# Where in its tiles the normed stream of a two-layer hybrid decoder stands: at the start, or at the end

## Chip, core and metric

The kernel runs on one core of one Trainium2 chip. The metric is the device time of one execution in microseconds, the median of the runs shown; the profile is of one execution, with a time of its own.

## What is computed

The reference is a trunk of two decoder layers over 16 learned tokens and 256 positions (272 in all), 2048 wide, in float32. Each layer is a normed mixer and a normed gated feed-forward block with a causal convolution of width 3, both with a residual.

```python
def reference(...):
    h = concat(meta, x)                        # 272 positions
    for i in range(2):
        hn = rmsnorm(h, norm_mix[i])
        mix = mixer_ab(hn, ...) if i % 2 == 0 else mixer_cd(hn, ...)
        h = h + mix
        h = h + conv_ffn(rmsnorm(h, norm_ffn[i]), ffn_w_up[i], ffn_dw[i], ffn_w_down[i])
    return rmsnorm(h, norm_final)[:, 16:]

def conv_ffn(h, w_up, dw, w_down):
    u = causal_dwconv(h @ w_up, dw)
    val, gate = u[..., :5632], u[..., 5632:]
    return (silu(gate) * val) @ w_down
```

## The kernel before

The stream is held transposed: 16 tiles `h[m]` of 128 channels by 272 positions. A product takes a block of 128 x 128 weights as the stationary operand and up to 272 positions as the moving one. For accuracy both operands are split into a rounded high part and a rest: the weights, which SP fetches in tiles `wf` of 1024 columns, become `wh` (ACT, line 161) and `wl` (DVE or POOL, line 163), 512 columns each; and each step of a product is three matmuls, high by high (line 170), high by low (line 171) and low by high (line 172), added up in PSUM. `gemm_steps` holds this loop. One output block of the up projections takes 16 steps, so 48 matmuls.

`Norm` makes the moving operand. `make_x(m)` writes the gain times `h[m]` in two halves, high (ACT, line 213) and low (DVE, line 214), into one stretch of a slab: `x` for the first 13 of the 16 tiles, the second slab `lt` for the last three where the norm is "wide". The factor of the root mean square comes in later, when a product is read out of PSUM. `xs()` hands the halves to the products.

The layout has a rule, since both operands of a matmul are read from SBUF at the same time. Call the *distance* the column (of 4 bytes) at which the moving operand begins, less the one at which a weight block begins, modulo 64. All weight tiles are multiples of 64 columns, so every weight block begins at the same place modulo 64 (32 in the built program).

- The three wide norms (`norm_mix0` for the first mixer, `norm_ffn0` and `norm_ffn1` for the up projections) give each half XW = 320 columns, five times 64. All halves then begin at the same place modulo 64 (16): distance 48 for every matmul. `norm_mix0` and `norm_ffn0` hold 272 positions, `norm_ffn1` holds 258.
- The tiles `act` that the down projections read (272 positions in layer 0, 256 in layer 1) are put at the same distance by a tile `gap` of 48 columns that nothing uses.
- `norm_mix1`, for the second mixer, isn't wide: its halves are 272 columns apart, and their distances rotate. For an even tile the high half is at 48 and the low at 0, for an odd one at 16 and 32. A part of the products of this mixer skips the first 12 or 14 columns of each half.

No table or planner sets the order of instructions; it is that of the code, queue by queue. In the long products PE has the next weights ready while it computes, and the products of one stage follow each other without a gap.

Of the kernel before, what the change touches and what calls it, by code (L numbers as in the profile page):

```python
# [21 lines left out]
T = NM + SEQ  # L22
# [73 lines left out]
def _body(ctx, tc, nc, A):  # L96
# [16 lines left out]
    def slab2(dt):  # L113
        return xpool.tile([P, 8 * T + 16], dt, tag="lt", name="lt")

    def pc(name, i=0, r0=0, r1=P):
        o = PO[name] + i
        return par[r0:r1, o:o + 1]
# [32 lines left out]
    def gemm_steps(w, g, xs, kt, acc, pool_lo=(), load=LOADK):  # L151
        for k0 in range(0, kt, load):
            nk = min(load, kt - k0)
            wf = wpool.tile([P, LOADK * P], F32, tag="wf", name="wf", bufs=NWF)
            nc.sync.dma_start(wf[:, :nk * P], w[g, :, k0 * P:(k0 + nk) * P])
            for s0 in range(0, nk, SUB):
                ns = min(SUB, nk - s0)
                src = wf[:, s0 * P:(s0 + ns) * P]
                wh = wpool.tile([P, SUB * P], F32R, tag="wh", name="wh")
                wl = wpool.tile([P, SUB * P], F32R, tag="wl", name="wl")  # L160
                last_hi[0] = S.copy(wh[:, :ns * P], src)  # L161
                eng = G if (k0 + s0) // SUB in pool_lo else V
                lo = eng.tensor_sub(wl[:, :ns * P], src, wh[:, :ns * P].bitcast(F32))  # L163
                if eng is V:
                    last_lo[0] = lo
                for k in range(ns):
                    kk = k0 + s0 + k
                    xh, xl = xs[kk]
                    a, b = wh[:, k * P:(k + 1) * P], wl[:, k * P:(k + 1) * P]
                    PE.matmul(acc, a, xh, start=kk == 0, stop=False)  # L170
                    PE.matmul(acc, a, xl, start=False, stop=False)  # L171
                    PE.matmul(acc, b, xh, start=False, stop=kk == kt - 1)  # L172
                yield

    def gemm(w, g, xs, n, pool_lo=()):
        acc = psA.tile([P, T], F32, tag="acc", name="acc")
        for _ in gemm_steps(w, g, xs, len(xs), acc[:, :n], pool_lo):
            tick()
        return acc[:, :n]
# [5 lines left out]
    def parts(t, c0, c1):  # L185
        return t[:, 0, c0:c1], t[:, 1, c0:c1]
# [10 lines left out]
    class Norm:  # L197
# [5 lines left out]
        def make_x(self, m):  # L203
            hm = h[m][:, self.c0:]
            if m == NXW and self.wide:
                self.slab2 = slab2(F32R)

            w, slab, i = XW if self.wide else T, xslab, m
            if self.wide and m >= NXW:
                slab, i = self.slab2, m - NXW  # L210
            x = slab[:, 2 * w * i:2 * w * (i + 1)].rearrange("p (a t) -> p a t", a=2)
            xh, xl = parts(x, 0, self.n)
            S.activation(xh, hm, AF.Copy, scale=pc(self.g, m))
            V.scalar_tensor_tensor(xl, hm, pc(self.g, m), xh.bitcast(F32), op0=ALU.mult, op1=ALU.subtract)
            self.x.append(x)
# [24 lines left out]
            self.rstd = r[:, self.c0:]  # L240

        def xs(self):
            return [parts(x, 0, self.n) for x in self.x]

    def add_h(m, acc, c0):
        V.tensor_add(h[m][:, c0:], h[m][:, c0:], acc)
# [8 lines left out]
    def mixer_ab(tp):  # L255
        nm = Norm("norm_mix0", 0, tp)
# [4 lines left out]
        xs = []  # L261
        first = [psb()[:, :T] for _ in range(2)]
        steps = [gemm_steps(A["ab_in"], g, xs, KD, first[g], (), SUB) for g in range(2)]
        for a, b in ((0, 2), (2, 4), (4, 8), (8, 12), (12, 16)):
            nc.sync.dma_start(h0[:, a:b], A["hT"][:, a:b])
            for m in range(a, b):
                nm.make_x(m)
            xs.extend(parts(x, 0, T) for x in nm.x[a:])
            if b % SUB == 0:
                for st in steps:  # L270
                    next(st)
# [139 lines left out]
    def ffn(layer, nm, gname, c1, tp, feed, spill=None):  # L411
        nxt = Norm(gname, c1, tp)
        c0 = nm.c0
        tp.tile([P, ACT_GAP], F32, name="gap", bufs=1)
        n = T - c0
        pad = 2 if layer == 0 else 0
        no = n if layer == 0 else n - 2
        xs = nm.xs()
        up, down, dw = A["up%d" % layer], A["down%d" % layer], "ffn_dw%d" % layer
        for half in range(2):  # L420
            act = []
            for j in range(NFH):
                i = half * NFH + j
                res = []
                for q in range(2):
                    ps = gemm(up, 2 * i + q, xs, n)
                    nm.finish()
                    u = tp.tile([P, T + 16], F32, tag="u%d" % q, name="u")
                    if pad:
                        G.memset(u[:, 0:2], 0.0)  # L430
                    V.tensor_mul(u[:, pad:pad + n], ps, nm.rstd)
                    c = tp.tile([P, T], F32, tag="c%d" % q, name="c")
                    conv3(c[:, :no], u, no, dw, q * NF + i)
                    res.append(c[:, :no])
                silu = S.activation(res[1], res[1], AF.Silu)  # L435
                G.tensor_mul(res[0], res[0], res[1])  # L436
                d = tp.tile([P, 2, ACT_W[layer]], F32R, tag="act", name="act", bufs=24)
                split(d, res[0], no)
                act.append(parts(d, 0, no))
            warm(AF.Sqrt, [silu])  # L440
            for m in range(KD):
                add_h(m, gemm(down, half * KD + m, act, no), T - no)
                if half:
                    feed(nxt, m)
                    if spill is not None:
                        nc.sync.dma_start(spill[:, m, :], h[m])
        return nxt
# [5 lines left out]
    with tc.tile_pool(name="ab", bufs=2) as tp:  # L453
        nm = mixer_ab(tp)
    hs = dpool.tile([P, KD, T], F32, name="hs")
    with tc.tile_pool(name="ffn0", bufs=2) as tp:
        nm = ffn(0, nm, "norm_mix1", 0, tp, feed_x, hs)
# [581 lines left out]
    with tc.tile_pool(name="cd", bufs=2) as tp:  # L1039
        nm = mixer_cd(tp, nm)  # L1040
    with tc.tile_pool(name="ffn1", bufs=2) as tp:
# [10 lines left out]
        nm = ffn(1, nm, "norm_final", NM, tp, feed_out)  # L1052
# [109 lines left out]
```

## Time and profile before

| | us |
|---|---|
| median of three runs | 2467.48 (2464.82 to 2470.11) |
| the profiled execution, its own time | 2466.42 |
| its span, first to last instruction | 2464.6 |
| PE busy | 2435.1 |
| DVE busy | 1783.4 |
| ACT busy | 1332.8 |
| POOL busy | 543.3 |

Busy time of PE counts the time from a matmul's start to its modelled end, and successive matmuls overlap: a matmul of 272 columns has a row of some 287 ns, while the next one starts some 123 ns after it. How fast a stage goes is therefore read from the timeline, as the time between two starts that are many matmuls apart, divided by the number of intervals.

### The profile page before, as it was taken

Reading aid. Unit: us, or ns where it says so; the run is one execution under the profiler, and the core shown is the slowest. Engines: PE = TensorE matmul, PEld = TensorE weight load, DVE = VectorE, ACT = ScalarE, POOL = GpSimd, SP = SyncE. Lnnn points to the kernel's source line nnn. Section 1 sums busy time; section 2 is a strip of 40 time slices with the busy share of each in tenths; the row PEclk is TensorE's granted clock in tenths of the full one; section 3 lists DMA queues with packets and bytes.
Section 4 is the critical chain, followed back from the end, with each engine's and each line's share of the span. In section 5 each row is a group of like instructions: output and inputs, shape, how many; then the busy total and the mean of one; then the engine's idle time right before and its main releaser. Section 6 shows DMA issues by size and latency. Waiting matters only on the chain.

```text
span 2464.6 us, 53380 instructions
## 1 busy us (share of the span) xinstructions
PE 2435.1 (99%) x20476; PEld 2378.0 (96%) x20476; DVE 1783.4 (72%) x3399; ACT 1332.8 (54%) x2573; POOL 543.3 (22%) x790
## 2 busy tenths in 40 slices
PE   8999999999999999999999999999999999999998
PEld 8999999999999999999899988899999999999998
DVE  8897897776546777667786678889777655777754
ACT  5444665555445555556645445546555545555553
POOL 5676140000000000121248044414000000000022
PEclk9999999999999999999999999999999999999999
DMA  6555555555655555666456342245555566555564
GB/s 219 192 177 180 171 174 179 179 180 176 175 181 181 180 180 178 183 194 192 132 160 174 122 130 87 93 141 181 184 184 184 181 192 194 185 183 180 177 197 149
DMA packets 130990, 423.94 MB, mean 172 GB/s; under 512 B 18832, under 2 KB 27216, under 8 KB 130736
## 3 DMA queue, kind: packets, MB, share of 16 engines
q1 hardware_dynamic: 129824, 417.99, 53.1%
q8 instruction: 161, 2.64, 0.4%
q0 software_dynamic: 912, 2.55, 0.4%
q14 instruction: 93, 0.76, 0.1%
HBM read 414.41 MB, written 5.93 MB: 171 GB/s over the span
## 4 chain that ended last, share of the span: by engine, by line
PE 95%; DVE 2%; ACT 1%; DMA 1%; POOL 0%; issue 0%; SPq 0%; DVEq 0%; ACTq 0%; POOLq 0%
PE acc L170 30%; PE acc L172 30%; PE acc L171 30%; PE ps L901 1%; DVE ps L296 1%; PE ps L935 1%; DVE wl L163 0%; PE ps L916 0%; PE ps L950 0%; PE ps L803 0%; PE ps L958 0%; PE ps L964 0%; DMA wf<-ab_in 0%; PE ps L697 0%; DMA h<-hT 0%
## 5 line engine op out<-in xcount | busy, mean ns | idle before, releaser
L161 ACT CAST wh<-wf 128x512 fp32r<-128x512 f32 (+1 forms) x1576 | 956.1, 611 | 919.0 <-PE acc L171 800.0
L163 DVE TENSOR_TENSOR wl<-wf,wh 128x512 fp32r<-128x512 f32 (+1 forms) x1465 | 1027.9, 706 | 480.9 <-ACT wh L161 423.8
L170 PE MATMUL acc<-x,wh 128*128 128x272 f32 (+2 forms) x3582 | 1034.9, 289 | 1.7 <-ACT wh L161 1.7
L172 PE MATMUL acc<-x,wl 128*128 128x272 f32 (+2 forms) x3582 | 1024.3, 286 | 2.5 <-DVE wl L163 2.3
L171 PE MATMUL acc<-x,wh 128*128 128x272 f32 (+2 forms) x3582 | 1023.0, 286 | 0.0
L170 PEld LDWEIGHTS acc<-x,wh 128*128 128x128 f32 x3582 | 677.4, 189 | 15.9 <-issue 7.5
L172 PEld LDWEIGHTS acc<-x,wl 128*128 128x128 f32 x3582 | 677.3, 189 | 5.2 <-DVE wl L163 3.5
L171 PEld LDWEIGHTS acc<-x,wh 128*128 128x128 f32 x3582 | 677.9, 189 | 1.1 <-issue 0.3
L171 PE MATMUL acc<-act,wh 128*128 128x272 f32 (+1 forms) x1408 | 396.1, 281 | 0.0
L170 PE MATMUL acc<-act,wh 128*128 128x272 f32 (+1 forms) x1408 | 396.1, 281 | 0.0
L172 PE MATMUL acc<-act,wl 128*128 128x272 f32 (+1 forms) x1408 | 396.1, 281 | 0.0
L170 PEld LDWEIGHTS acc<-act,wh 128*128 128x128 f32 x1408 | 264.8, 188 | 0.0
L171 PEld LDWEIGHTS acc<-act,wh 128*128 128x128 f32 x1408 | 264.8, 188 | 0.0
L172 PEld LDWEIGHTS acc<-act,wl 128*128 128x128 f32 x1408 | 264.8, 188 | 0.0
L436 POOL TENSOR_TENSOR c<-c 128x272 f32<-128x272 f32 (+1 forms) x88 | 66.5, 756 | 639.9 <-ACT c L435 639.9
L170 PE MATMUL acc<-lt,wh 128*128 128x272 f32 (+1 forms) x642 | 183.4, 286 | 0.0
L171 PE MATMUL acc<-lt,wh 128*128 128x272 f32 (+1 forms) x642 | 182.9, 285 | 0.0
L172 PE MATMUL acc<-lt,wl 128*128 128x272 f32 (+1 forms) x642 | 182.9, 285 | 0.0
L163 POOL TENSOR_TENSOR wl<-wf,wh 128x512 fp32r<-128x512 f32 x111 | 149.1, 1353 | 54.2 <-ACT wh L161 53.5
L430 POOL MEMSET u<- 128x2 f32 x88 | 8.6, 100 | 573.1 <-DVE c L252 566.5
L172 PEld LDWEIGHTS acc<-lt,wl 128*128 128x128 f32 x642 | 121.7, 190 | 0.0
L171 PEld LDWEIGHTS acc<-lt,wh 128*128 128x128 f32 x642 | 121.6, 189 | 0.0
(316 smaller groups left out, 2858.2 us busy)
## 6 DMA issues: line engine op xcount, KB each, us to landing
wf<-up SPq DMA_DIRECT2D x352, 512.0 KB, 3.5
wf<-down SPq DMA_DIRECT2D x128, 512.0 KB, 3.7
wf<-cd_in SPq DMA_DIRECT2D x100, 512.0 KB, 3.6
wf<-ab_in SPq DMA_DIRECT2D x76, 512.0 KB, 3.7
wf<-down SPq DMA_DIRECT2D x64, 384.0 KB, 3.3
wf<-ab_out_s SPq DMA_DIRECT2D x16, 512.0 KB, 3.5
wf<-ab_out_a SPq DMA_DIRECT2D x16, 512.0 KB, 3.9
wf<-cd_out_o SPq DMA_DIRECT2D x16, 512.0 KB, 3.5
```

Source lines behind the costliest of these rows:

```text
L161: last_hi[0] = S.copy(wh[:, :ns * P], src)
L163: lo = eng.tensor_sub(wl[:, :ns * P], src, wh[:, :ns * P].bitcast(F32))
L170: PE.matmul(acc, a, xh, start=kk == 0, stop=False)
L171: PE.matmul(acc, a, xl, start=False, stop=False)
L172: PE.matmul(acc, b, xh, start=False, stop=kk == kt - 1)
L296: tap = V.scalar_tensor_tensor(c if t == 30 else run, ap[:, t:t + T], pc("conf_dw", 31 * i + t), run, op0=ALU.mult, op1=ALU.add)
L430: G.memset(u[:, 0:2], 0.0)
L436: G.tensor_mul(res[0], res[0], res[1])
L901: PE.matmul(gv[:, :128], bkc, t[r, h0], start=True, stop=True)
L935: PE.matmul(wy[H[h0], 0:64], t[:, h0, 0:64], sv[:, h0], start=True, stop=True)
```

## The change

The moving operand of the three wide norms stands at the end of its 320 columns, not at their start. `parts(x, a, b)` takes the columns a to b of both halves, and n is the number of positions that the norm holds (272 or 258).

```diff
@@ make_x
-            xh, xl = parts(x, 0, self.n)
+            xh, xl = parts(x, w - self.n, w)
             S.activation(xh, hm, AF.Copy, scale=pc(self.g, m))
             V.scalar_tensor_tensor(xl, hm, pc(self.g, m), xh.bitcast(F32), op0=ALU.mult, op1=ALU.subtract)
@@ xs
-            return [parts(x, 0, self.n) for x in self.x]
+            return [parts(x, x.shape[-1] - self.n, x.shape[-1]) for x in self.x]
@@ mixer_ab
-            xs.extend(parts(x, 0, T) for x in nm.x[a:])
+            xs.extend(nm.xs()[a:])
```

With 272 positions the first column moves by 48 columns (192 bytes), from distance 48 to distance 32; its columns from the 17th on, the last 256, begin at distance 48. With 258 positions the first column moves by 62 columns (248 bytes), to distance 46, and again the last 256 begin at distance 48. For `norm_mix1` w and n are both 272, and nothing moves. Tiles, their addresses and their sizes stay as they are, and so does the sequence of instructions on every engine (19130 listed ones on PE, 2637 on DVE, 1546 on ACT, 460 on POOL, 238 on SP): the change alters the start column of operands and nothing else.

## Rows read from the trace of the kernel before

**Rows 1.** The page: busy us (share) xinstructions; chain that ended last.
```profile
PE 2435.1 (99%) x20476; PEld 2378.0 (96%) x20476; DVE 1783.4 (72%) x3399; ACT 1332.8 (54%) x2573; POOL 543.3 (22%) x790
...
PE 95%; DVE 2%; ACT 1%; DMA 1%; POOL 0%; issue 0%; SPq 0%; DVEq 0%; ACTq 0%; POOLq 0%
PE acc L170 30%; PE acc L172 30%; PE acc L171 30%; PE ps L901 1%; DVE ps L296 1%; PE ps L935 1%; DVE wl L163 0%; PE ps L916 0%; PE ps L950 0%; PE ps L803 0%; PE ps L958 0%; PE ps L964 0%; DMA wf<-ab_in 0%; PE ps L697 0%; DMA h<-hT 0%
```

**Rows 2.** Waits of PE, longest first: us in total, times, longest us.
```profile
PE ps L170 <- ACT wh L161: 7.2, 2, 6.9
PE acc L172 <- DVE wl L163: 2.3, 4, 1.4
```

**Rows 3.** Stretches of 30 us: busy us of each engine (xinstructions), PEclk, DMA share, GB/s.
```profile
200.00:230.00 30.00, 30.00 (x246) 30.00 (x245) 24.27 (x50) 14.54 (x25) 21.70 (x17) 1.00 0.54 179
900.00:930.00 30.00, 30.00 (x246) 30.00 (x245) 21.45 (x39) 15.99 (x29) 2.05 (x7) 1.00 0.53 177
1800.00:1830.00 30.00, 30.00 (x253) 30.00 (x252) 21.63 (x39) 16.42 (x30) 1.48 (x2) 1.00 0.55 181
2000.00:2030.00 30.00, 30.00 (x268) 30.00 (x266) 16.59 (x29) 14.07 (x24) 0.00 (x0) 1.00 0.68 194
2200.00:2230.00 30.00, 30.00 (x251) 30.00 (x250) 21.16 (x38) 17.01 (x31) 1.91 (x3) 1.00 0.54 179
```

**Rows 4.** Timeline (start, duration us), PE, up projection of layer 0, 97 intervals.
```profile
900.02 0.29 PE L172 MATMUL acc<-lt,wl 128*128 128x272 f32 x1
...
911.98 0.28 PE L170 MATMUL acc<-lt,wh 128*128 128x272 f32 x1
```

**Rows 5.** Timeline, PE, up projection of layer 1, first half, 99 intervals.
```profile
1800.09 0.28 PE L172 MATMUL acc<-lt,wl 128*128 128x258 f32 x1
...
1811.97 0.28 PE L172 MATMUL acc<-lt,wl 128*128 128x258 f32 x1
```

**Rows 6.** Timeline, PE, up projection of layer 1, second half, 99 intervals.
```profile
2200.00 0.28 PE L172 MATMUL acc<-x,wl 128*128 128x258 f32 x1
...
2211.96 0.28 PE L172 MATMUL acc<-x,wl 128*128 128x258 f32 x1
```

**Rows 7.** Timeline, PE, down projection of layer 1, 105 intervals.
```profile
2000.08 0.28 PE L171 MATMUL acc<-act,wh 128*128 128x256 f32 x1
...
2011.98 0.28 PE L171 MATMUL acc<-act,wh 128*128 128x256 f32 x1
```

**Rows 8.** Timeline, PE, mixer of layer 1, rotating distances, 272 columns, 28 intervals.
```profile
1154.01 0.29 PE L170 MATMUL acc<-x,wh 128*128 128x272 f32 x1
...
1157.50 0.29 PE L171 MATMUL acc<-x,wh 128*128 128x272 f32 x1
```

**Rows 9.** Timeline, PE, mixer of layer 1, first 14 columns skipped, 32 intervals.
```profile
1211.27 0.28 PE L171 MATMUL acc<-x,wh 128*128 128x258 f32 x1
...
1215.12 0.28 PE L170 MATMUL acc<-x,wh 128*128 128x272 f32 x1
```

**Rows 10.** Weight loads by form: 2000 to 2030, 900 to 930, 1800 to 1830 us.
```profile
L170 PEld LDWEIGHTS acc<-act,wh 128*128 128x128 f32 x89 | 16.7, 188 | 0.0
...
L170 PEld LDWEIGHTS acc<-x,wh 128*128 128x128 f32 x66 | 12.4, 188 | 0.0
...
L170 PEld LDWEIGHTS acc<-x,wh 128*128 128x128 f32 x68 | 13.0, 191 | 0.0
```

**Rows 11.** Groups by form, whole span: busy us, mean ns, idle before, releasers.
```profile
L213 ACT ACTIVATE x<-h,par 128x272 fp32r<-128x272 f32 x42 | 21.0, 520 | 11.4 <-DVE h L246 5.9 <-DMA h<-hT 4.1
...
L214 DVE SCALAR_TENSOR_TENSOR x<-h,par,x 128x272 fp32r<-128x272 f32 x42 | 31.0, 753 | 5.0 <-ACT x L213 5.0
```

## The prediction

> **What bounds the kernel now.** I read the page's busy table and chain first. PE is busy for 99% of the span and 95% of the chain that ended last is PE, nearly all of it the three matmul lines 170, 171 and 172 [rows 1]. In the whole execution PE waits for other engines only in single pieces, the largest group being 7.2 us [rows 2]. So the time is a sum of intervals between the starts of successive matmuls, and an edit that moves no instruction can only act through that interval. A matmul's mean duration doesn't give it, because matmuls overlap: rows last 276 to 288 ns, but start every 113 to 125 ns. I therefore take the interval from the timeline, as first start to last start divided by the number of intervals. The granted clock is 1.00 in every stretch used, the 2.4 GHz level [rows 3], where 256 columns stream in 106.7 ns, 258 in 107.5 and 272 in 113.3.
>
> The intervals, in order of the stages [rows 4 to 9]:
> - 272 columns, up projection of layer 0: from 900.02 to 911.98 there are 97 intervals, 123.3 ns each, 10.0 above the streaming time [rows 4].
> - 258 columns, up projection of layer 1, first half: 1800.09 to 1811.97, 99 intervals, 120.0 ns, 12.5 above [rows 5].
> - the same in the second half: 2200.00 to 2211.96, 99 intervals, 120.8 ns, 13.3 above [rows 6].
> - 256 columns, down projection of layer 1: 2000.08 to 2011.98, 105 intervals, 113.3 ns, 6.7 above [rows 7].
>
> All four read their moving columns from the same distance to the weights (48 columns, counted modulo 64, from the start of a weight block to the first column). The two columns between 256 and 258 thus cost 6.7 to 7.5 ns [rows 5 to 7], where their streaming is 0.8. The weight load that runs beside the matmul lasts 188 ns beside 256 and 272 columns and 191 beside 258 [rows 10]: something delays these reads, and it isn't a semaphore. That is what the change can touch: if 272 and 258 paid only the 6.7 of 256, they would start every 120.0 and 114.2 ns.
>
> Two more stretches show other distances. In layer 1's mixer the normed tiles are 272 columns wide, so their halves rotate through all four distances (48, 0, 16, 32). There 272 columns take 124.6 ns (1154.01 to 1157.50, 28 intervals) [rows 8], and 258 columns that begin 14 columns into the tile take 120.3 ns (1211.27 to 1215.12, 32 intervals) [rows 9].
>
> **The change part by part.** It removes and adds no instruction, no wait and no transfer; sequences on all engines are the same. Two things change their address.
>
> (a) *The writers*, lines 213 and 214: 48 pairs on ACT and DVE, of the same shapes, at 520 and 753 ns for 272 columns [rows 11]. They write as many columns 192 or 248 bytes further on. 32 of the 48 pairs stand beside the last output projection of a mixer, where PE has work queued. The 16 of the first normalization stand at the start of the program, where the longest wait of PE is [rows 2]. A change of 5% in both would be 16 x 1.27 x 0.05 = 1 us; I take 0, and ±1 for the bounds.
>
> (b) *The readers*. Matmuls that read the moved tiles: 40 products of 16 steps and 3 matmuls in the first mixer (1920) and 88 x 16 x 3 = 4224 in the up projection of layer 0, so 6144 with 272 columns; and 4224 with 258 columns in that of layer 1. The rest (mixer of layer 1, both down projections, the output projections) reads tiles that don't move. For 272 columns the first column goes from distance 48 to distance 32. For 258 it goes from 48 to 46, in the middle of what was a 16-column step, so that the two extra columns now stand ahead of 256 columns at the common distance.
>
> No row shows all matmuls of a stage at distance 32 or 46, so the price is bounded from both sides.
> - 272 columns. Below: 120.0 ns, the extra cost of the 256-column rows. Above: 126.7, as far above the present 123.3 as 120.0 is below. I take the nearest row, the rotating stretch, in which one row in six is at distance 32: 124.6. That is +1.35 x 6144 = **+8.3 us**, with ends -20.5 and +20.5.
> - 258 columns. Below: 114.2 (-6.2 on the mean of 120.0 and 120.8, which is 120.4). Above: 123.7, the same 3.3 step. I take the rotating stretch whose rows also begin 14 columns past a 16-column step, 120.3, and leave the lock between the two halves open, so 120.6: +0.2 x 4224 = **+0.8 us**, ends -26.4 and +13.9.
>
> Cover: DVE has 21 to 24 busy of 30 us in these stages and the transfers 53 to 55% [rows 3], so a PE that gets 5% faster would still be fed; nothing hides a slower one, since PE has no idle time to give.
>
> Sum: 0 + 8.3 + 0.8 = +9.1 us on the profiled execution's 2466.4, that is 2475.5; the median of the runs shown is 1.06 us above that execution, so **2476.5**.
>
> **A rule weighed.** Rows 7 against rows 5 show that two columns more cost eight times their streaming time at an unchanged distance, and rows 8 against rows 4 that 272 columns cost 1.3 ns more when the distance rotates. The Trainium skill, "TensorE: Matmul & The Clock Gate", section "Step-by-step: what each phase is for", says the opposite of a cost by place: PE reads SBUF through two independent ports, one for the moving operand and one for weight loads, so a weight load takes no bandwidth from a running matmul. By it the sum would be 0 and the time 2467.5; this is the third rival below. The trace agrees with it only as far as both run at once.
>
> **The rivals.**
> 1. *Forecast: place matters, and the new place is no better than the mixed ones.* The present 48 is the one distance for which a stage of 272 columns runs in a regular beat of 123.3; leaving it costs what the rotating rows cost. Against it: in those rows each matmul follows one at another distance, so they don't show a beat at 32 alone. 2476.5, from +2 to +20 us. Chance 0.41.
> 2. *The tail is the cost (faster).* The present distance suits 256 columns [rows 7]; whatever comes behind the 256th column meets the weight load a further time. Ahead of them it doesn't. For: 256 to 258 is a step, not a slope [rows 5, 7], and the weight load grows with it at 258 [rows 10]. Against: beside 272 columns the load doesn't grow, and in rows 9 the 258 columns already begin 14 past a step, with their partial step ahead, and still take 120.3. It decides if 272 columns fall below 122.5 ns (-5 us). If only 272 gains: 2466.4 + 1.1 - 20.5 = 2447; if only 258: 2441; if both: 2421. Chance 0.29.
> 3. *Nothing.* The extra cost goes with the number of 16-column steps (16 for 256, 17 for both 258 and 272), which the move leaves as it is, or place doesn't matter. 2467.5 ± 4.9. Chance 0.20.
> 4. *Both stages fall out of their beat.* The first half of layer 1 runs in an even 120.0 and the second in 120.8 with the same addresses [rows 5, 6], so the beat isn't fixed by the addresses alone and can be lost: 126.7 and 123.7 give 2467.5 + 20.5 + 13.9 = 2502. Chance 0.10.
>
> **How the numbers follow.** Under 0.2% (4.9 us) either way can't be told from no change for this kernel. Slower: nearly all of the first (0.39) and the fourth: 0.49. Faster: 0.29. Within: 0.20 and the small end of the first: 0.22. The range reaches down to 2444, which holds the case where 272 alone gains and leaves out the larger gains (about 0.12), and up to 2496, which leaves out the full loss in both widths (about 0.08). The likeliest case's own range is 2469 to 2488.
>
> **What would show it.** In the profile after, the same stretches of the up projections, read as starts per interval: about 124.6 in layer 0 and 120.6 in layer 1 if I am right, 120.0 and 114.2 for the second rival, 123.3 and 120.4 for the third. The down projection of layer 1 must stay at 113.3 and the mixer of layer 1 near 124.6, since nothing there moved. I am wrong if the difference lies outside those 10368 matmuls, or if PE's waits in the start of the program change.

## The result: slower by 1.1%, three times the forecast loss

| | before | after |
|---|---|---|
| median, us | 2467.16 (2464.82 to 2470.11) | 2496.16 (2492.60 to 2496.76) |
| ratio, 95% interval | | 1.0111 [1.0098, 1.0124] |
| profiled execution / its span | 2466.42 / 2464.6 | 2492.6 / 2490.8 |

The forecast was 2476.5, so +9.1; the loss is 29.0, and the time lies at the very upper end of the range. The spans differ by 26.2 us.

The page of the changed kernel, busy time (share) x instructions and the chain that ended last:

```profile
span 2490.8 us, 53380 instructions
PE 2463.4 (99%) x20476; PEld 2406.8 (97%) x20476; DVE 1783.6 (72%) x3399; ACT 1336.5 (54%) x2573; POOL 542.6 (22%) x790
...
PE 97%; DVE 1%; ACT 1%; POOL 0%; DMA 0%; issue 0%; SPq 0%; DVEq 0%; POOLq 0%; ACTq 0%
```

Against [rows 1], PE has the same 20476 instructions and is busy 28.3 us longer; DVE, ACT and POOL stay within 4 us. PE's longest waits (total, times, longest) answer [rows 2]:

```profile
PE ps L170 <- ACT wh L161: 6.8, 1, 6.8
PE acc L171 <- DVE halves L183: 1.9, 1, 1.9
```

7.2 us became 6.8, so no wait of PE was added; the 1.9 us for DVE stands in the kernel before too. Most of the loss is in the pace. The stretches of 30 us of [rows 3], with the number of matmuls in brackets behind the first 30.00:

```profile
200.00:230.00 30.00, 30.00 (x239) 30.00 (x238) 24.93 (x52) 13.29 (x24) 20.97 (x17) 1.00 0.50 170
900.00:930.00 30.00, 30.00 (x239) 30.00 (x239) 20.96 (x38) 16.34 (x31) 2.82 (x8) 1.00 0.53 176
1800.00:1830.00 30.00, 30.00 (x252) 30.00 (x251) 21.64 (x39) 17.41 (x33) 2.23 (x3) 1.00 0.56 185
2000.00:2030.00 30.00, 30.00 (x257) 30.00 (x257) 15.48 (x26) 13.73 (x24) 0.00 (x0) 1.00 0.65 192
2200.00:2230.00 30.00, 30.00 (x252) 30.00 (x251) 21.12 (x39) 17.43 (x32) 2.24 (x3) 1.00 0.54 177
```

The granted clock is 1.00 in all of them, as before. With 272 columns 246 matmuls became 239. With 258 the 253 and 251 became 252. The surprise is the fourth row: 268 became 257 in the down projection of layer 1, whose tiles `act` didn't move by a byte.

The timeline (start, duration) gives the intervals. In order: up projection of layer 0 (answers [rows 4]), 94 intervals; up projection of layer 1 in its two halves ([rows 5, 6]), 99 each; down projection of layer 1 ([rows 7]), 101.

```profile
900.08 0.29 PE L172 MATMUL acc<-x,wl 128*128 128x272 f32 x1
...
911.98 0.29 PE L170 MATMUL acc<-x,wh 128*128 128x272 f32 x1
```
```profile
1800.01 0.28 PE L170 MATMUL acc<-x,wh 128*128 128x258 f32 x1
...
1811.89 0.28 PE L170 MATMUL acc<-x,wh 128*128 128x258 f32 x1
```
```profile
2230.01 0.29 PE L170 MATMUL acc<-x,wh 128*128 128x258 f32 x1
...
2241.90 0.28 PE L170 MATMUL acc<-x,wh 128*128 128x258 f32 x1
```
```profile
2015.02 0.28 PE L171 MATMUL acc<-act,wh 128*128 128x256 f32 x1
...
2026.91 0.28 PE L170 MATMUL acc<-act,wh 128*128 128x256 f32 x1
```

These are 11.90/94 = 126.6 ns (123.3 before), 11.88/99 = 120.0 (120.0), 11.89/99 = 120.1 (120.8) and 11.89/101 = 117.7 (113.3).

Taking the time from the first start of each stage to the first start of the next, in both traces, accounts for the span. The pace in ns is that of a gap-free part of the stage:

| stage | matmuls | ns before | ns after | change, us |
|---|---|---|---|---|
| first mixer, input, 272 columns | 1920 | 123.33 | 126.67 | +3.9 |
| first mixer, output (`halves`), not moved | 768 | 123.33 | 123.33 | +1.6 |
| up projection, layer 0 | 4224 | 123.33 | 126.67 | +14.1 |
| down projection, layer 0, not moved | 2112 | 123.33 | 123.34 | 0.0 |
| mixer, layer 1, not moved | 3168 | | | -0.6 |
| up projection, layer 1, first half | 2112 | 120.01 | 120.00 | 0.0 |
| the same, second half | 2112 | 120.83 | 120.00 | -1.8 |
| down projection, layer 1, **not moved** | 2112 | 113.35 | 117.78 | **+9.4** |

The sum is +26.6; what follows the last product is 0.3 us shorter. The first mixer gained only 3.9 us where 1920 matmuls at 3.33 ns more make 6.4, because the starts that wait at the beginning of the program cost about 2.4 us less in this execution. This beginning varies: in the six traced kernels whose first mixer isn't moved, that stage takes 242.6 to 247.2 us.

The +1.6 of the stage `halves` is neither pace nor wait but the clock. PE waits 1.9 us for DVE there in both kernels; behind it the granted clock is 1.00 before, and 0.50 (the 1.2 GHz level) for 3.4 us after, with some 15 starts 227 ns apart. First before, then after:

```profile
258.00:260.00 2.00, 2.00 (x19) 1.00 0.33 66
```
```profile
262.00:264.00 2.00, 2.00 (x10) 0.50 0.34 88
```

The same fall stands in the two further traced kernels below in which the 272 columns are moved, and in none of the six in which they aren't; why is not shown.

So two questions are open: why 272 columns came out at the upper end, and why a stage slowed whose addresses stayed.

### The profile page after: what moved, and what is told of

Its sections match the earlier page's. It is cut to its first block, busy times and chain, and to the rows that moved or that the text cites. A ratio compares the mean times of both kernels' runs of the same rounds, so it can differ in the third digit from the quotient of the medians.

```text
span 2490.8 us, 53380 instructions
## 1 busy us (share of the span) xinstructions
PE 2463.4 (99%) x20476; PEld 2406.8 (97%) x20476; DVE 1783.6 (72%) x3399; ACT 1336.5 (54%) x2573; POOL 542.6 (22%) x790
## 4 chain that ended last, share of the span: by engine, by line
PE 97%; DVE 1%; ACT 1%; POOL 0%; DMA 0%; issue 0%; SPq 0%; DVEq 0%; POOLq 0%; ACTq 0%
PE acc L170 31%; PE acc L172 30%; PE acc L171 30%; PE ps L901 1%; PE ps L935 1%; PE ps L916 0%; PE ps L950 0%; PE ps L803 0%; PE ps L958 0%; DMA h<-hT 0%; PE ps L964 0%; DVE wl L163 0%; PE ps L697 0%; PE ps L818 0%; PE ps L816 0%
```

## Experiments

Before these runs three theories stood for the second question. *By address*: the place alone sets the pace. *By entry*: a stage can run in several steady beats at the same addresses, and what stands ahead of it chooses. *By traffic*: the other engines' reads and writes do it. The first prices also had to be taken on their own, without the rest of the kernel.

**Matmuls alone.** One tile holds weights and moving operands; the three matmuls of a step repeat for 32 steps at a chosen width and distance, and ACT reads the sum after each stretch. The bench kernels compute nothing of the reference.

```diff
...
+for s in range(32):
+    ...                                        # a, b: weight blocks; xh, xl: moving operands
+    PE.matmul(acc[:, :n], a, xh, start=s == 0, stop=False)
+    PE.matmul(acc[:, :n], a, xl, start=False, stop=False)
+    PE.matmul(acc[:, :n], b, xh, start=False, stop=s == 31)
```

> A bench of matmuls alone, nothing of the reference is computed: 512 columns to begin with, then stretches of 96 matmuls in the pattern of the products (high by high, high by low, low by high) for 256, 258, 264, 272 and 288 columns at distances 0, 8, ... 56 (named a to h in the order run), each stretch after a pause; then two widths with different distances for the two halves; then stretches that follow each other without a pause. Theory A (the place sets the beat, the place alone): at distance 48 the starts come every 113.3 ns with 256 columns, 120.0 to 120.8 with 258 and 123.3 with 272, at distance 32 every 126.7 with 272, and a stretch of 256 at 48 has 113.3 whatever stretch it follows. Theory B (the place sets a few possible beats, and the entry chooses among them): the 256-column stretch at 48 has 113.3 after some stretches and 117.8 after 258 columns at 46. Theory C (no effect of the place by itself; other engines' traffic makes it): all distances alike within 0.5 ns in this bench.

No other engine worked beside these matmuls, DMA moved 1 GB/s, the granted clock was 1.00, and the kernel's paces were there: 272 columns 123.3 ns at distance 48 and 126.7 at 32, 258 columns 120.8 at 48 and 120.0 at 46, 256 columns 113.3 at 48. So traffic isn't needed for any of them. Two stretches of 256 columns at distance 48 that follow 272 columns without a pause, first behind distance 32, then behind 48 (timeline of the bench, 52 and 50 intervals):

```profile
977.04 0.28 PE L120 MATMUL acc<-big 128*128 128x256 f32 x1
...
982.93 0.28 PE L121 MATMUL acc<-big 128*128 128x256 f32 x1
```
```profile
1001.06 0.28 PE L121 MATMUL acc<-big 128*128 128x256 f32 x1
...
1006.95 0.28 PE L120 MATMUL acc<-big 128*128 128x256 f32 x1
```

5.89/52 = 113.3 ns and 5.89/50 = 117.8 ns: the same tile, the same distance, and the two paces of the down projection. Behind 258 columns at 46 and at 48 the bench gave 113.3 both times, so which entry gives which pace doesn't carry over from the bench to the kernel. In this bench halves at two distances have a price of their own: 124.4 ns for 272 columns at 48 and 0, and 124.5 at 16 and 32, near the 124.6 of [rows 8], where these two pairs alternate. No distance in steps of 8 was below 48's 113.3 and 123.3 for 256 and 272.

**The move for the norms with 272 columns only.**

```diff
...
+            xh, xl = self.half(x)
...
+            return [self.half(x) for x in self.x]
+
+        def half(self, x):
+            o = x.shape[-1] - self.n if self.g != "norm_ffn1" else 0
+            return parts(x, o, o + self.n)
```

> The move made for norm_mix0 and norm_ffn0 alone (272 columns); norm_ffn1 stays at the start of its tiles. Theory A and B: the 6144 matmuls of the two stages start every 126.7 ns instead of 123.3, +20 us, and layer 1 is as in the kernel before: up projection 120.0 to 120.8, down projection 113.3; 2487 us. Rival (the slower down projection of layer 1 comes from the whole program's shift in time, not from its own stage): down projection 117.8, 2496 us.

2484.47 us, ratio 1.0059 [1.0041, 1.0077]. The timeline in the up projection of layer 0 (94 intervals) and the down projection of layer 1 (105):

```profile
900.02 0.29 PE L172 MATMUL acc<-lt,wl 128*128 128x272 f32 x1
...
911.93 0.29 PE L170 MATMUL acc<-lt,wh 128*128 128x272 f32 x1
```
```profile
2020.04 0.28 PE L170 MATMUL acc<-act,wh 128*128 128x256 f32 x1
...
2031.94 0.28 PE L170 MATMUL acc<-act,wh 128*128 128x256 f32 x1
```

126.7 ns, and 113.3: the wide stages slow down by themselves, and layer 1 keeps its old pace in every stage (120.0, 120.8, 113.35). The profiled execution was 2492.13, above this run's median, because its first mixer took 7.2 us longer than in the changed kernel: PE waited once for DVE's sums, 4.9 us, and behind that the granted clock was 0.50 from 35 to 40 us, with starts 227 ns apart. The steady intervals of the stage are the same 126.67.

**The move for the norm with 258 columns only** (the condition reversed, `if self.g == "norm_ffn1" else 0`).

> The move made for norm_ffn1 alone (258 columns). Theory B (the beat of the down projection is inherited from the stage ahead of it): up projection 120.0 in both halves (-1.8 us), down projection 117.8 at unmoved tiles (+9.3 us), 2474.5 us. Theory A or the rival of the run before: down projection 113.3, 2465 us.

2474.82 us, ratio 1.0033 [1.0016, 1.0051]. Up projection 120.0 in both halves (-1.8 us), down projection (101 intervals):

```profile
2005.04 0.28 PE L171 MATMUL acc<-act,wh 128*128 128x256 f32 x1
...
2016.93 0.28 PE L170 MATMUL acc<-act,wh 128*128 128x256 f32 x1
```

11.89/101 = 117.7, so +9.4 us in a stage that this edit doesn't touch. The two parts, 0.59% and 0.33%, make up most of the 1.11%, within their intervals.

**All distances, and many entries, alone.** The same bench with each stretch behind a pause: 258 columns at all 64 distances, 272 at 33 to 63, 256 at 41 to 55; then the three widths at one distance behind three matmuls of 16 to 272 columns.

> The bench again, nothing of the reference is computed: 258 columns at all 64 distances, 272 at 33 to 63, 256 at 41 to 55 (96 matmuls each, after a pause), and then stretches of 96 matmuls of 256, 272 and 258 columns at distance 48, each entered through a single matmul of 16, 32, ... 272 columns. Theory B (few beats, chosen by the entry): the 256-column stretches take either 113.3 or 117.8 ns, nothing between, according to the entry; 272 and 258 may have a second beat too. Theory A (the place alone): one value for each width. For the table: 258 columns should be lowest near distance 30 (117.8 ns in the first bench), and 256 at 48.

258 columns take 120 to 122 ns at most distances and 115.6 at 7, 11 and 63; the 48 of the kernel before (120.8) and the 46 after (120.0) are both ordinary. That 256 columns are lowest at 48 was missed: this stretch took 117.8, and 116.7 stood at 51 and 55. For 272 columns 123.3 is the lowest of that list, at 35, 40, 43, 44, 47, 48, 59 and 63. The entries: 256 columns at 48 took 113.3 behind 10 of 17 entries and 117.8 behind 7, with nothing between. 272 columns took 123.3 behind 16 and 126.7 behind one, and 258 took 120.8 behind 14 and 120.0 behind 3, which are the two paces of layer 1's up projection in the kernel before. What stands ahead isn't the whole of it: over both benches, six stretches of 256 columns at 48 with nothing but a pause ahead took 113.3 four times and 117.8 twice.

**Another entry in the changed kernel.** One small float32 matmul of 64 columns ahead of each pass of layer 1's down projection.

```diff
             warm(AF.Sqrt, [silu])
+            if layer:
+                PE.matmul(psb()[:, :64], ones, cc("ones", 64), start=True, stop=True)
```

> The changed kernel with one small matmul more (64 columns of float32, its result unused) ahead of each of the two passes of the down projection of layer 1, where addresses are the same before and after the change. Theory B (the entry chooses the beat): the entry has another timing, and the stage may run at 113.3 ns instead of 117.8, 2487 us; if it stays at 117.8, the entry is not shown to choose. Rival (the move itself slows the unmoved stage, by what stands in the moved tiles): 117.8 whatever stands ahead, 2496 us.

2494.93 us, ratio 1.0119 [1.0090, 1.0148]. The down projection stayed at 117.78. Alone this decides nothing: a different entry may choose the same beat.

**The same small matmul in the kernel before**, where no tile is moved.

> The kernel before with the same small matmul ahead of each pass of the down projection of layer 1. Theory B: this stage can fall to 117.8 ns without any tile being moved, 2477 us, or stay at 113.3, 2467 us. Rival: 113.3, 2467 us.

2473.03 us, ratio 1.0020 [1.0009, 1.0032]. The down projection in its first half (101 intervals) and its second (105):

```profile
2005.07 0.28 PE L171 MATMUL acc<-act,wh 128*128 128x256 f32 x1
...
2016.97 0.28 PE L170 MATMUL acc<-act,wh 128*128 128x256 f32 x1
```
```profile
2385.05 0.28 PE L170 MATMUL acc<-act,wh 128*128 128x256 f32 x1
...
2396.95 0.28 PE L170 MATMUL acc<-act,wh 128*128 128x256 f32 x1
```

117.8 and 113.3 ns in one execution, at the addresses of the kernel before and with the same added matmul ahead of both. The first half costs 4.8 us more, which is most of the loss of this run (6.0 between medians). This is what settles the second question: address alone doesn't set the pace, and a change of the entry is enough to change it. As the same matmul stands ahead of both halves, the entry is more than which instruction comes last. A kernel falls the same way from execution to execution, as far as times tell: all eight here took 2470.9 us or more and all eight of the kernel that moves the 258 columns alone 2472.3 or more, against a median of 2467 to 2468 for the kernel before.

**258 columns at distance 30** (the kernel before, `norm_ffn1` moved by 46 columns), which the first bench put at 117.8 ns.

> The kernel before with norm_ffn1 alone moved, by 46 columns (258 columns at distance 30, the lowest place for 258 in the first bench). Theory A and B: up projection of layer 1 at 117.8 ns instead of 120.0 and 120.8, -11 us; the down projection at 113.3 or 117.8 by its entry, so 2456 or 2466 us. Rival (the bench doesn't carry over to the kernel): 120 to 121 ns, no gain.

2465.03 us, ratio 0.9993 [0.9979, 1.0008]: no difference. The up projection ran at 120.0 (99 intervals):

```profile
1800.06 0.28 PE L172 MATMUL acc<-lt,wl 128*128 128x258 f32 x1
...
1811.94 0.28 PE L172 MATMUL acc<-lt,wl 128*128 128x258 f32 x1
```

A miss. Two bench stretches of 96 matmuls, both at 117.8, didn't give the pace of a stage of 2100 at the same distance. Why wasn't found out; a second beat at 30 that neither bench stretch fell into would do it.

**Several entries per distance**: each of twelve pairs of width and distance behind eleven different entries.

> The bench, nothing of the reference is computed: stretches of 96 matmuls, each entered through three matmuls of 24, 48, ... 264 columns, at the places that matter: 272 columns at distances 32 (the changed kernel), 40, 47, 63, 35; 258 columns at 46 (the changed kernel), 63, 7, 11, 23, 55, 4. If the move of the 272-column tiles costs by the place and not by an unlucky entry, 272 at 32 has 126.7 ns for nearly all entries, against 123.3 at 48 (16 of 17 entries in the bench before). If the entry alone decides, 123.3 turns up at 32 about as often as 126.7. 258 at 46: 120.0 for nearly all entries. A place at which 258 columns start every 115.6 to 117 ns whatever the entry is a candidate for the kernel (63, 7 and 11 had 115.6 with the entry of the second bench).

272 columns at 32 took 126.7 ns behind all eleven, and 123.3 behind all eleven at 35, 40, 47 and 63. The timeline inside a stretch at 32 (62 intervals) and one at 47 (64):

```profile
100.03 0.29 PE L121 MATMUL acc<-big 128*128 128x272 f32 x1
...
107.88 0.29 PE L120 MATMUL acc<-big 128*128 128x272 f32 x1
```
```profile
349.99 0.28 PE L120 MATMUL acc<-big 128*128 128x272 f32 x1
...
357.88 0.28 PE L121 MATMUL acc<-big 128*128 128x272 f32 x1
```

7.85/62 = 126.6 and 7.89/64 = 123.3 ns. So the first question is one of place: distance 32 has that pace behind every entry tried, while 48 has it behind one in 17. 258 columns at 7, 11 and 63 took 115.6 behind all eleven, at 46 120.0 behind all, and at 55 either of two paces.

**258 columns at distances 63 and 7 in the kernel** (before, `norm_ffn1` moved by 15 or by 23 columns).

> The kernel before with norm_ffn1 alone moved by 15 columns (258 columns at distance 63: 115.6 ns for all eleven entries of the bench). If the bench carries over: up projection of layer 1 from 120.0 and 120.8 to 115.6 ns, -20.5 us; the down projection at 113.3 (2447 us) or, by its entry, 117.8 (2456 us). If not (as with the move by 46, where the bench's 117.8 became 120.0): 120.0, 2465 us.

> The same with a move by 23 columns (distance 7: 115.6 ns for all eleven entries). The same three outcomes: 2447, 2456 or 2465 us; it differs from the move by 15 only if the entry of the down projection falls the other way.

2448.56 us, ratio 0.9923 [0.9910, 0.9937], and 2446.27, ratio 0.9918 [0.9904, 0.9932]: both faster than either kernel. The up projection of the first (103 intervals):

```profile
1800.08 0.28 PE L172 MATMUL acc<-lt,wl 128*128 128x258 f32 x1
...
1811.98 0.28 PE L170 MATMUL acc<-x,wh 128*128 128x258 f32 x1
```

11.90/103 = 115.5 ns. The stage gives back 9.4 us in the first half and 11.2 in the second, and the down projection behind it kept 113.3. The cover in the prediction held: in layer 1's feed-forward block PE waited for no weights; its longest wait, for the first weights of the program, was 8.2 us (6.9 before).

**Which distance counts.** The bench with its weights begun 0, 2, 8, 16, 32 or 48 columns further on, the moving operand at fixed distances behind them, some of them 64 apart.

> Matmuls alone, 32 steps of three for each stretch after a pause; nothing of the reference is computed. Weight blocks begin 0, 16, 32, 48, 8 or 2 columns past a multiple of 64, and the moving operand begins a fixed distance behind the weights: 32, 48, 96 or 112 for 272 columns; 7, 63, 71, 127 or 48 for 258. Theory of the relative distance counted modulo 64: every stretch of 272 columns starts every 126.7 ns at 32 and 96, and 123.3 ns at 48 and 112, wherever the weights begin; 258 columns take 115.6 ns at 7, 63, 71 and 127. Rival one, the absolute column modulo 64 counts: with weights 16 further on, distance 32 reads from column 48 and takes 123.3, and distance 48 reads from column 0 and takes 125.3. Rival two, the period is 128: 96 and 112, or 71 and 127, differ from 32 and 48, or 7 and 63, by over 2 ns. If some stretches differ by an entry of their own, single ones jump by 3 to 4 ns without a pattern.

The timeline with weights 16 columns on, at distance 32 (30 intervals) and at 48 (31):

```profile
100.09 0.29 PE L119 MATMUL acc<-big 128*128 128x272 f32 x1
...
103.89 0.29 PE L119 MATMUL acc<-big 128*128 128x272 f32 x1
```
```profile
113.10 0.29 PE L119 MATMUL acc<-big 128*128 128x272 f32 x1
...
116.92 0.28 PE L120 MATMUL acc<-big 128*128 128x272 f32 x1
```

3.80/30 = 126.7 and 3.82/31 = 123.2 ns. Over all of them, 32 and 96 took 126.7 wherever the weights began (10 of 10 stretches), 48 and 112 took 123.3 in 8 of 10, and 7, 63, 71 and 127 took 115.6 with 258 columns (12 of 12). So it is the distance between the two operands that counts, and at these distances 64 more makes no difference. Of the other two, both at 48, one with the weights not moved took 126.7, another case of two paces at one place, and the one with the weights 2 columns on took 124.5 in the mean.

## Why the prediction came out as it did

1. **What bounds the kernel: right.** PE is 99% busy in both, no wait of over 1 us was added, and nearly all the difference is in the interval between starts at a clock of 1.00. The prediction had no term for the clock, and 1.6 us came from it, in a stage that didn't move. The two writers cost nothing that can be seen.

2. **The 272-column term: mis-sized.** It was taken at 124.6 ns, +8.3 us. It measured 126.67, the stated upper end: 3.33 x 6144 = 20.5 us; the stages grew by 18.0, since the start of the program was about 2.4 us shorter. The failing step is the choice of row. In [rows 8] one matmul in six reads at distance 32 and each follows one at another distance, so they hold a mixture. The first rival gave that itself as what spoke against it, and the forecast then used the row's mean as a pace all the same. By the first bench the row is near the price of two halves at unlike distances, 124.4 and 124.5 ns, which says nothing of 32 alone. The upper end, 126.7, "as far above the present 123.3 as 120.0 is below", hit by luck: nothing in the trace pointed at 126.7.

3. **The 258-column term: right in being small, wrong in sign.** +0.8 forecast, -1.8 measured. Both halves now run at 120.0, and what is gained is the 120.8 of the second half. The bench has both paces at 48 and, behind eleven entries, only 120.0 at 46.

4. **The missing term: the down projection of layer 1.** The prediction said that it "must stay at 113.3 [...] since nothing there moved", and put any loss outside the moved matmuls among the signs that it was wrong. It went to 117.78: 4.43 ns x 2112 = +9.4 us, a third of the loss. The step that failed is from "its addresses stay" to "its pace stays". The rows to see it in were there: [rows 5] and [rows 6] show 120.0 and 120.8 at the same addresses. The prediction read them as two beats for one stage, in the fourth rival alone, and didn't ask which other stages have two.

5. **The rivals.** The tail (rival 2) is refuted: neither 120.0 for 272 columns nor 114.2 for 258 appeared, and the added columns ahead of the 256 cost as much as behind, or more. No effect (rival 3) is refuted twice, by the changed kernel and by the bench, where nothing but the place differs between 126.7 and 123.3. That also speaks against the rule weighed there (the Trainium skill, "TensorE: Matmul & The Clock Gate", "Step-by-step: what each phase is for"): with two ports that don't disturb each other the place would not matter, and here it does, by 3.3 ns a matmul. Falling out of the beat (rival 4) is real, but it struck the one stage that the rival didn't name, and 272 columns at 32 didn't fall out of a beat: 126.7 is what that place gives behind every entry tried.

6. **The size.** Terms as measured: +18.0 (272 columns) + 1.6 (the clock in `halves`) - 1.8 + 9.4 - 0.6 = +26.6 on the profiled execution, and 29.1 with the 272 columns at their pace alone (20.5), near the 29.0 between the medians. The direction came out right; of its +9.1, nearly all was the 272-column term at less than half its size.

What stays open: which accesses of the two operands collide, and what distinguishes the entries that lead to 113.3 from those that lead to 117.8. The pace of the stage ahead doesn't: behind 120.0 the down projection took 113.3 in the first half of the kernel before and at distance 30, and 117.8 in the changed kernel. That data, traffic or the wait for PSUM play no part was not tried in the kernel itself; the bench shows only that both paces arise without other engines at work.

## What to carry to other kernels

Where matmuls follow each other without a wait, read each stage's pace as starts per interval from the timeline, and ask of every stage whether it has been seen in more than one pace; a stage downstream of an edit can change its pace though none of its operands moved. The pace of a new placement is measured with matmuls alone in a few microseconds, but behind several entries and not one, since a stretch can sit in a beat that the kernel doesn't take. A row that mixes placements bounds nothing about one of them.

## What the hardware showed that was not expected

- At one place a stage has one or two steady paces: at distance 48 113.3 or 117.8 ns for 256 columns, 120.0 or 120.8 for 258 and 123.3 or 126.7 for 272. Over all distances the pace of 258 columns spreads from 115.6 to 122.2, and over distances 33 to 63 that of 272 from 123.3 to 130.0, at a granted clock of 1.00.
- 256 columns at the same tile and distance run steadily in either of two paces, for a whole stage (1056 matmuls, 4.7 us apart); one small matmul ahead was enough to change which.
- Two columns more at a good distance cost little: 258 at distance 63 or 7 take 115.6 ns against 113.3 for 256. The 120.0 that the prediction took as the price of the step from 256 to 258 is the price of an ordinary distance.
